# Gate and up products of a 512-token swiglu as seven block products instead of eight

## The chip, the cores and the metric

The kernel runs on one core of a Trainium2 chip. Its time is device microseconds from the first to the last instruction of one execution; several executions of a kernel are compared by their median. Five engines take part: TensorE (PE) multiplies, VectorE (DVE) and ScalarE (ACT) do the elementwise work, SyncE (SP) issues the loads, GpSimd (POOL) does next to nothing here. Each engine runs its own instructions in order and waits on semaphores for the others.

## What is computed

Two blocks of a diffusion transformer over 256 latent and 256 context tokens of width 1024, in fp32. Cut to its core:

```python
def _modulate(t, g, shift, scale):
    return _rms(t, g) * (1 + scale) + shift

def _swiglu(h, w13, w2):
    gte, up = jnp.split(h @ w13, 2, axis=-1)
    return (jax.nn.silu(gte) * up) @ w2

mod = silu(c) @ mod_w[i] + mod_b[i]             # nine vectors; another nine from c_ctx
lat = lat + 0.5 * mod[0, 2] * _swiglu(_modulate(lat, ...), ffn_w13[i, 0], ffn_w2[i, 0])
lat = lat + mod[1, 2] * mixer(_modulate(lat, ...))   # i = 0: short convolution, i = 1: attention
lat = lat + 0.5 * mod[2, 2] * _swiglu(_modulate(lat, ...), ffn_w13[i, 1], ffn_w2[i, 1])
```

The context tokens go through the same steps with their own modulation, except behind the attention. So there are three swiglus over 512 tokens, called ffn(0,0), ffn(0,1) and ffn(1,0) after layer and place, and a last one, ffn(1,1), over the 256 latent tokens. The hidden width is 2816, that is 22 tiles of 128.

## The kernel before

All activations lie with features on the partitions and tokens along the free dimension: `x` is 8 tiles (k tiles) of 128 features by 512 tokens, the latent stream in columns 0 to 255, the context in 256 to 511. An fp32 operand is split into two float32r parts: ACT copies the high part (L90), DVE subtracts it for the low part (L91). Each product is then three matmuls (`mm3`, L105 to L107): high by high, high by low, low by high.

A swiglu goes through the 22 pairs of a gate tile (`pg`) and an up tile (`pu`) in two halves of 11. For a pair SP loads 1 MB of `w13` into one of three raw buffers (`wr`), ACT and DVE split it (`wh`, `wl`), and PE runs 8 k tiles x 2 x 3 matmuls over 512 columns. Then ACT takes the silu of the gate (L357), DVE multiplies by up (L359, `gm`), and both split the product into `gh` and `gl`, an operand of the second product. After 11 pairs `project` runs the 8 output tiles of `w2` over these 11 tiles and adds them, times the gate `G`, to `x` (L296). With the last half's output, squares and sums for the norm are made as tiles come (`tail_norm`); the last two output tiles are done a stream at a time (`late`), so that the norm of the latent tokens (L222, L225, L226: `t`, `hh`, `hl`) runs behind the products of the context. Where a swiglu begins with no pair done, its first two pairs are interleaved by stream, in products of 256 columns.

The modulation vectors of all chunks but the first two are made on DVE: a job (`mod_job`) loads 1 MB of `modT` and runs four (two where only the latent stream is needed) multiply-and-reduce instructions (L128, output `junk`). There are 64 jobs in a list. `tick()` takes the next one after every other pair and every other output tile, and after each tile of the convolution; what is needed and not yet done is forced where it is first read (`mod_ready`), as by the gate of a block. The instructions stand on each engine in an order that the scheduler of the framework makes from the program's order and its own estimates; it is fixed when the kernel is built.

```python
        hi = wp.tile([P, 2048], F32R, name=nm("wh"), tag="wh", bufs=3)
        lo = wp.tile([P, 2048], F32R, name=nm("wl"), tag="wl", bufs=3)
        ...
        ticks[0] += 1
        if jobs and ticks[0] % every == 0:
            mod_job(*jobs.pop(0))
```

## Time and profile before

| | |
|---|---|
| median of 3 runs | 1619.42 us (1618.96 to 1620.31) |
| span of the profiled execution | 1618.8 us |
| PE busy | 1607.0 us (99%) |
| DVE busy | 996.7 us (62%) |
| ACT busy | 535.2 us (33%) |
| loads | 245 MB, 152 GB/s over the span |

The stages by the trace: start 0 to 62 us, ffn(0,0) to 394, convolution and its projection to 604, ffn(0,1) to 936 and its last tiles to 968, ffn(1,0) to 1300, then attention, output projection and ffn(1,1) to the end. A row of the timeline gives the start, the length, the engine, line, operation, output and inputs of an instruction; a row of waits gives who waited for whom, the total, the number of times and the longest; a row of windows gives, for a stretch, its length, then each engine's busy time and the number of its instructions, the granted clock of TensorE, the share of the DMA engines and GB/s. Matmul records overlap: what one costs is the distance to the start of the next.

### The profile page before, as it was taken

To read this page: it belongs to the slowest core of one execution; us is meant where nothing else is said; L and a number is where in the kernel's file an instruction comes from. 1 tells how busy PE (TensorE), PEld (TensorE's weight loads), DVE (VectorE), ACT (ScalarE), POOL (GpSimd) and SP (SyncE) were. 2 spreads that over 40 slices of the span, in tenths; PEclk is the share of its full clock that TensorE was granted. 3 is DMA by queue.
4 is the path that set the end of the run, shared out by engine and by line. 5 is a ranking of instruction groups with operands and counts; after the bars stand their busy time and mean duration, and the time that the engine had idled before them with its cause. 6 is when DMAs were issued, how large, how long until landed. Compare 5 with 4: busy or idle time off the path is not lost.

```text
span 1618.8 us, 21098 instructions
## 1 busy us (share of the span) xinstructions
PE 1607.0 (99%) x8718; PEld 1390.3 (86%) x8718; DVE 996.7 (62%) x1601; ACT 535.2 (33%) x811; POOL 0.2 (0%) x4
## 2 busy tenths in 40 slices
PE   9999999999999999999999999999999999999999
PEld 6888888889888898888888898888888899989999
DVE  4975565566978795557554595445443577855554
ACT  4422122224322252222222342222222356553442
POOL 0000000000000000000000000000000000000000
PEclk9999999999999999999999999999999999999999
DMA  8543544333544434345343345335433432244643
GB/s 311 213 165 124 192 163 156 132 116 131 182 163 175 177 136 152 118 138 204 130 148 124 135 154 182 124 130 207 152 124 120 161 129 84 106 156 137 218 169 103
DMA packets 40560, 248.49 MB, mean 153 GB/s; under 512 B 5392, under 2 KB 7184, under 8 KB 16656
## 3 DMA queue, kind: packets, MB, share of 16 engines
q1 hardware_dynamic: 38016, 245.38, 42.9%
q10 hardware_dynamic: 2448, 1.76, 0.4%
q8 instruction: 68, 1.11, 0.3%
q14 instruction: 28, 0.23, 0.0%
HBM read 244.77 MB, written 1.05 MB: 152 GB/s over the span
## 4 chain that ended last, share of the span: by engine, by line
PE 95%; DVE 3%; ACT 1%; DMA 1%; issue 0%; ACTq 0%; SPq 0%; DVEq 0%
PE py L105 10%; PE py L106 10%; PE py L107 10%; PE pg L105 9%; PE pg L106 9%; PE pu L105 9%; PE pu L106 8%; PE pg L107 8%; PE pu L107 8%; PE pr L434 1%; PE pv L105 1%; PE pv L107 1%; PE pv L106 1%; PE pb L107 1%; PE pb L105 1%; PE pc L107 1%
## 5 line engine op out<-in xcount | busy, mean ns | idle before, releaser
L90 ACT ACTIVATE wh<-wr 128x1024 fp32r<-128x1024 f32 (+2 forms) x358 | 326.8, 952 | 344.7 <-PE py L106 210.1
L91 DVE TENSOR_TENSOR wl<-wr,wh 128x1024 fp32r<-128x1024 f32 (+2 forms) x358 | 384.3, 1095 | 24.1 <-ACT wh L90 23.0
L128 DVE CUSTOM_DVE_ANT_0 junk<-wr,scbc,modb 128x1024 bf16<-128x1024 f32 x236 | 293.1, 1280 | 145.2 <-DMA wr<-in_modT 145.2
L107 PE MATMUL py<-gh,wl 128*128 128x512 f32 (+1 forms) x770 | 267.1, 347 | 0.0
L105 PE MATMUL py<-gh,wh 128*128 128x512 f32 (+1 forms) x770 | 267.1, 347 | 0.0
L106 PE MATMUL py<-gl,wh 128*128 128x512 f32 (+1 forms) x770 | 266.9, 347 | 0.0
L105 PE MATMUL pg<-hh,wh 128*128 128x512 f32 (+1 forms) x736 | 262.3, 356 | 2.0 <-ACT hh L225 2.0
L106 PE MATMUL pg<-hl,wh 128*128 128x512 f32 (+1 forms) x736 | 261.5, 355 | 0.0
L105 PE MATMUL pu<-hh,wh 128*128 128x512 f32 (+1 forms) x736 | 261.5, 356 | 0.0
L106 PE MATMUL pu<-hl,wh 128*128 128x512 f32 (+1 forms) x736 | 261.4, 355 | 0.0
L107 PE MATMUL pu<-hh,wl 128*128 128x512 f32 (+1 forms) x736 | 261.3, 355 | 0.0
L107 PE MATMUL pg<-hh,wl 128*128 128x512 f32 (+1 forms) x736 | 261.3, 355 | 0.0
L357 ACT ACTIVATE sg<-pg 128x512 f32<-128x512 f32 (+1 forms) x88 | 47.9, 545 | 551.1 <-PE pg L107 551.1
L359 DVE TENSOR_TENSOR gm<-sg,pu 128x512 f32<-128x512 f32 (+1 forms) x88 | 54.5, 620 | 225.0 <-ACT sg L357 213.4
L105 PEld LDWEIGHTS py<-gh,wh 128*128 128x128 f32 x770 | 145.2, 189 | 18.2
L107 PEld LDWEIGHTS py<-gh,wl 128*128 128x128 f32 x770 | 145.2, 189 | 18.0
L106 PEld LDWEIGHTS py<-gl,wh 128*128 128x128 f32 x770 | 145.2, 189 | 18.0
L105 PEld LDWEIGHTS pg<-hh,wh 128*128 128x128 f32 x736 | 139.4, 189 | 22.5 <-ACT hh L225 2.7
L105 PEld LDWEIGHTS pu<-hh,wh 128*128 128x128 f32 x736 | 139.4, 189 | 19.5
L106 PEld LDWEIGHTS pg<-hl,wh 128*128 128x128 f32 x736 | 139.1, 189 | 19.2
L107 PEld LDWEIGHTS pu<-hh,wl 128*128 128x128 f32 x736 | 139.0, 189 | 19.3
L107 PEld LDWEIGHTS pg<-hh,wl 128*128 128x128 f32 x736 | 139.0, 189 | 19.3
(155 smaller groups left out, 1608.8 us busy)
## 6 DMA issues: line engine op xcount, KB each, us to landing
wr<-in_w SPq DMA_DIRECT2D x88, 1024.0 KB, 4.8
wr<-in_modT SPq DMA_DIRECT2D x67, 1024.0 KB, 4.8
wr<-in_w SPq DMA_DIRECT2D x64, 704.0 KB, 4.1
wr<-in_cw_cx SPq DMA_DIRECT2D x8, 1024.0 KB, 4.8
wr<-in_mod SPq DMA_DIRECT2D x5, 1024.0 KB, 7.0
wr<-in_cw_b SPq DMA_DIRECT2D x4, 1024.0 KB, 4.7
wr<-in_cw_out SPq DMA_DIRECT2D x4, 1024.0 KB, 4.8
wr<-in_wq SPq DMA_DIRECT2D x4, 1024.0 KB, 4.8
```

What stands on the lines that cost most here:

```text
L90: nc.scalar.activation(out=hi, in_=src, func=AF.Copy)
L91: nc.vector.tensor_tensor(out=lo, in0=src, in1=hi.bitcast(F32), op=ALU.subtract)
L105: nc.tensor.matmul(ps, wh, mh, start=first, stop=False)
L106: nc.tensor.matmul(ps, wh, ml, start=False, stop=False)
L107: nc.tensor.matmul(ps, wl, mh, start=False, stop=last)
L128: nc.vector.tensor_tensor_reduce(out=junk, in0=raw[:, j * D : j * D + D], in1=scbc[:, v, :], scale=1.0, scalar=modb[:, l, col : col + 1], ...
L357: nc.scalar.activation(out=sg[:, :n], in_=pp[0][:, :n], func=AF.Silu)
L359: nc.vector.tensor_tensor(out=gm[:, :n], in0=sg[:, :n], in1=pp[1][:, :n], op=ALU.mult)
L434: nc.tensor.matmul(pr[:2, :S], sccol[:, k, :], raw[:, k * S : k * S + S], start=(k == 0), stop=(k == KT - 1),)
```

## The change

61 of the 66 pairs of the three 512-token swiglus (all but the first three of ffn(0,0) and the first of each of the others, which is done in two halves of 256 columns with the `head` of the next two pairs between them) are seen as a product of two by two blocks. The weight blocks are A11 (gate) and so on: rows are gate (1) and up (2), columns are k tiles 0 to 3 and 4 to 7; the activation blocks B are k tiles by stream. The Strassen-Winograd scheme needs seven block products, each of 4 k tiles x 3 matmuls x 256 columns. `Pair` makes the weight sums S1 to S4 on DVE (L519, L525, L527) from the loaded fp32 and splits A11 with A12, S1 with S2, S3 with S4 (1024 columns each) and A22 (512). The sums T1 to T4 of the activations are made once per swiglu on DVE (`Blocks.sums`; in ffn(0,0) `FirstBlocks.sums`, L341 to L345), from an fp32 copy of the normed activations that the norm now also writes.

PE runs a pair in pieces, interleaved with the pair before: `head` (two products, with A11 and A12), `five` (S1 by T1), then `seven` of the pair before (S3 by T3), `six` (S2 by T2, S4 by B22), then `four` of the pair before (A22 by T4). Partial results stay in two PSUM tiles `p` and `q`. ACT copies them to SBUF where an addend is needed (L545, L551, L555), DVE adds (L557 for the gate; L562 for up, back into PSUM), ACT takes the silu (L558), and DVE multiplies (L568).

The 22 pairs go in thirds of 8, 7 and 7, so `w2` is loaded and projected in three parts. A projection starts with three output tiles at once, whose last two k tiles wait for the last pair's `seven` and `four`, which stand between them. Weights are split into half tiles of 1024 columns with four buffers. Modulation jobs are no longer taken in the pairs: `tick(ev)` adds a share for each output tile (0.5, in ffn(1,0) 0.9; in the convolution 1.2 a tile) and takes whole jobs. The normed activations and the attention's turned tiles live in 16 buffers of 1024 columns (`hop`).

On DVE, the steady loop of the pairs in the second half of ffn(0,0) before, and in the second third now (`gm`: the pair's product, `gl`: its low part, `wl`: low parts of weights, `ws`: weight sums, `w4l`: that of A22, `p`: the up sum, `sg`: the gate sum):

```order
L359 TENSOR_TENSOR gm_1696<-sg_1694,pu_1645 128x512
L91 TENSOR_TENSOR wl_1856<-wr_1853,wh_1855 128x1024
L91 TENSOR_TENSOR gl_1643<-gm_1696,gh_1642 128x512
L91 TENSOR_TENSOR wl_1856<-wr_1853,wh_1855 128x1024
L128 ISA junk_1993,mod_4_1700<-wr_1985,scbc,modb 128x1024
L128 ISA mod_4_1700 128x1
L359 TENSOR_TENSOR gm_1773<-sg_1771,pu_1722 128x512
L91 TENSOR_TENSOR wl_1922<-wr_1919,wh_1921 128x1024 x2
L91 TENSOR_TENSOR gl_1720<-gm_1773,gh_1719 128x512
```

After the change, at the same place:

```order
L562 TENSOR_TENSOR p_1987<-p_1987,gm_2027 128x256
L92 TENSOR_TENSOR wl_2217<-ws_2209,wh_2216 128x1024
L92 TENSOR_TENSOR wl_2222<-ws_2209,wh_2221 128x1024
L557 TENSOR_TENSOR sg_2110<-q_2109,sg_2110 128x512
L519 TENSOR_TENSOR ws_2330<-wr_2328 128x2x512
L568 TENSOR_TENSOR gm_2027<-sg_1989,p_1987 128x512
L92 TENSOR_TENSOR w4l_2226<-wr_2207,w4h_2225 128x512
L525 TENSOR_TENSOR ws_2330<-wr_2328,ws_2330 128x512
L92 TENSOR_TENSOR gl_2191<-gm_2027,gh_2190 128x512
L527 TENSOR_TENSOR ws_2330<-wr_2328,ws_2330 128x512
L92 TENSOR_TENSOR wl_2332<-wr_2328,wh_2331 128x1024
```

The modulation is gone from the loop; three weight sums, two more low parts and two sums of results have come into it, eleven rows to a pair.

On DVE, in the projection after the first part of ffn(0,0) (`x`: an output tile's addition; `junk`: modulation):

```order
L296 SCALAR_TENSOR_TENSOR x<-py_1282,G_1215,x 128x256 x2
L91 TENSOR_TENSOR wl_1419<-wr_1416,wh_1418 128x768
L91 TENSOR_TENSOR wl_1419<-wr_1416,wh_1418 128x640
L296 SCALAR_TENSOR_TENSOR x<-py_1326,G_1215,x 128x256 x2
L91 TENSOR_TENSOR wl_1473<-wr_1470,wh_1472 128x768
L91 TENSOR_TENSOR wl_1473<-wr_1470,wh_1472 128x640
L128 ISA junk_1560,mod_3_1263<-wr_1558,scbc,modb 128x1024
...
L128 ISA junk_1562,mod_3_1263<-wr_1558,scbc,modb 128x1024
...
L128 ISA junk_1564,mod_3_1263<-wr_1558,scbc,modb 128x1024
...
L128 ISA junk_1566,mod_3_1263<-wr_1558,scbc,modb 128x1024
...
L296 SCALAR_TENSOR_TENSOR x<-py_1380,G_1215,x 128x256 x2
```

After the change, at the same place:

```order
L417 SCALAR_TENSOR_TENSOR x<-py_1447,G_1418,x 128x256 x2
L138 ISA junk_1476,mod_3_1427<-wr_1474,scbc,modb 128x1024
...
L92 TENSOR_TENSOR wl_1487<-wr_1484,wh_1486 128x1024
L138 ISA junk_1478,mod_3_1427<-wr_1474,scbc,modb 128x1024
...
L92 TENSOR_TENSOR wl_1518<-wr_1484,wh_1517 128x1024
L138 ISA junk_1480,mod_3_1427<-wr_1474,scbc,modb 128x1024
...
L138 ISA junk_1482,mod_3_1427<-wr_1474,scbc,modb 128x1024
...
L138 ISA junk_1550,mod_3_1427<-wr_1548,scbc,modb 128x1024
...
L417 SCALAR_TENSOR_TENSOR x<-py_1490,G_1418,x 128x256 x2
L138 ISA junk_1552,mod_3_1427<-wr_1548,scbc,modb 128x1024
...
L138 ISA junk_1554,mod_3_1427<-wr_1548,scbc,modb 128x1024
...
L92 TENSOR_TENSOR wl_1561<-wr_1558,wh_1560 128x1024
```

Before, the four rows of a job stand behind the weights of every second output tile. Now rows of jobs stand around every low part of the weights (`wl_1487` and the others); eight jobs lie in this projection, of which the gate `G` forces the first four.

On DVE, at the start of the attention (`wl_9527` before and `wl_12935` now are the first query weights):

```order
L296 SCALAR_TENSOR_TENSOR x<-py_9257,G_7894,x 128x256 x2
L91 TENSOR_TENSOR wl_9527<-wr_9524,wh_9526 128x1024 x2
L192 TENSOR_TENSOR acc_9034<-acc_9034,sq_9293 128x256
...
L296 SCALAR_TENSOR_TENSOR x<-py_9315,G_7894,x 128x256
...
L296 SCALAR_TENSOR_TENSOR x<-py_9353,G_7894,x 128x256
L210 RECIPROCAL ri_9416<-rs_9414 128x2
L222 SCALAR_TENSOR_TENSOR t_9420<-x,A_9390,ss_9409 128x256
...
L226 SCALAR_TENSOR_TENSOR hl_6937<-t_9420,mod_3_6182,hh_6936 128x256
...
L296 SCALAR_TENSOR_TENSOR x<-py_9393,G_7894,x 128x256
```

After the change, at the same place:

```order
L138 ISA junk_12911,mod_8_12900<-wr_12907,scbc,modb 128x1024
...
L231 SCALAR_TENSOR_TENSOR t_12827<-x,A_12803,ss_12816 128x256
...
L242 SCALAR_TENSOR_TENSOR hl_9154<-t_12827,mod_3_10288,hh_9153 128x256
...
L417 SCALAR_TENSOR_TENSOR x<-py_12806,G_10284,x 128x256
...
L417 SCALAR_TENSOR_TENSOR x<-py_12859,G_10284,x 128x256
...
L242 SCALAR_TENSOR_TENSOR hl_9160<-t_12881,mod_3_10288,hh_9159 128x256
L138 ISA junk_12915,mod_8_12900<-wr_12913,scbc,modb 128x1024
...
L92 TENSOR_TENSOR wl_12935<-wr_12932,wh_12934 128x1024
L138 ISA junk_12917,mod_8_12900<-wr_12913,scbc,modb 128x1024
...
L92 TENSOR_TENSOR wl_12937<-wr_12932,wh_12936 128x1024
```

The query weights stood ahead of the norm's rows; now they stand behind the norm of the latent stream and behind three rows of the last modulation chunk, and the fourth and fifth come next.

The diff, cut to its core:

```diff
-HALF = NM // 2
+THIRDS = (8, 7, 7)
...
-    gp = ctx.enter_context(tc.tile_pool(name="gp", bufs=12))
+    hop = ctx.enter_context(tc.tile_pool(name="hop", bufs=16))
+    gp = ctx.enter_context(tc.tile_pool(name="gp", bufs=8))
...
+    def half():
+        return tuple(
+            wp.tile([P, 1024], F32R, name=nm(t), tag=t, bufs=4) for t in ("wh", "wl")
+        )
...
-    def tick(every=2):
...
-        ticks[0] += 1
-        if jobs and ticks[0] % every == 0:
+    owed = [0.0]
+    def tick(share):
+        owed[0] += share
+        while jobs and owed[0] >= 1:
+            owed[0] -= 1
             mod_job(*jobs.pop(0))
...
+    class Blocks:
...
+        def block(self, s, hf, A, B, ri, fine=False):
+            raw = self.raw[hf, s] = hot("hr", F32)
+            hi, lo = self.t["B", hf, s] = hot("bh"), hot("bl")
+            for i in range(4):
+                k = 4 * hf + i
+                c = slice(i * S, i * S + S)
+                t = scaled(s, k, A, ri)
+                nc.scalar.activation(
+                    out=raw[:, c], in_=t, func=AF.Identity, bias=B[:, k, s : s + 1]
+                )
+                if fine and i % 2:
+                    c = slice((i - 1) * S, (i + 1) * S)
+                    split(hi[:, c], lo[:, c], raw[:, c])
+            if not fine:
+                split(hi, lo, raw)
...
+        def sums(self):
+            r = self.raw
+            b11, b12, b21, b22 = r[0, 0], r[0, 1], r[1, 0], r[1, 1]
+            tt = nc.vector.tensor_tensor
+            def keep(key, src):
+                hi, lo = self.t[key] = hot("th"), hot("tl")
+                split(hi, lo, src)
+            tt(out=b11, in0=b12, in1=b11, op=ALU.subtract)
+            keep("T1", b11)
+            tt(out=b12, in0=b22, in1=b12, op=ALU.add)
+            tt(out=b22, in0=b22, in1=b11, op=ALU.add)
+            keep("T2", b22)
+            tt(out=b21, in0=b21, in1=b22, op=ALU.subtract)
+            keep("T3", b12)
+            keep("T4", b21)
...
+        nf = 3 if between else 2
+        w2 = [ws(m) for m in range(nf)]
+        p2 = [psum("py") for _ in range(nf)]
+        cut = nk - 2 if between else nk - 1
+        for i in range(nf):
+            products(p2[i], w2[i], range(cut), 0, tot)
+            if i < len(between):
+                between[i]()
+        if between:
+            for i in range(nf):
+                products(p2[i], w2[i], (nk - 2,), 0, tot)
+        for i in range(nf):
+            products(p2[i], w2[i], (nk - 1,), 0, tot)
+            finish(i, p2[i], 0, tot, gate, tail)
+            tick(ev)
...
+    class Pair:
+        def __init__(self, src, h):
+            self.h = h
+            raw = load_raw(src)
+            a21, a22, a11, a12 = (raw[:, i * T2 : i * T2 + T2] for i in range(4))
+            tt = nc.vector.tensor_tensor
+            sm = wp.tile([P, 2048], F32, name=nm("ws"), tag="ws", bufs=1)
+            s1, s2, s3, s4 = (sm[:, i * T2 : i * T2 + T2] for i in range(4))
+            self.w = {}
+            def keep(keys, src):
+                hi, lo = half()
+                split(hi, lo, src)
+                for i, key in enumerate(keys):
+                    self.w[key] = [t[:, i * T2 : i * T2 + T2] for t in (hi, lo)]
+            keep(("A11", "A12"), raw[:, 1024:])
+            tt(
+                out=sm.rearrange("p (a b c) -> p a b c", a=2, b=2)[:, :, 0, :],
+                in0=a21.unsqueeze(1).to_broadcast([P, 2, T2]),
+                in1=raw[:, T2 : 3 * T2].rearrange("p (a c) -> p a c", a=2),
+                op=ALU.subtract,
+            )
+            tt(out=s2, in0=a11, in1=s1, op=ALU.subtract)
+            keep(("S1", "S2"), sm[:, :1024])
+            tt(out=s4, in0=a12, in1=s2, op=ALU.subtract)
+            keep(("S3", "S4"), sm[:, 1024:])
+            self.w["A22"] = [
+                wp.tile([P, T2], F32R, name=nm(t), tag=t, bufs=2) for t in ("w4h", "w4l")
+            ]
+            split(*self.w["A22"], a22)
+        def prod(self, ps, wk, hk, first=True):
+            for k in range(4):
+                w = tuple(t[:, k * P : k * P + P] for t in self.w[wk])
+                mm3(ps, w, self.h.blk(hk, k), first and k == 0, k == 3, True)
+        def head(self):
+            p, q = psum("p"), psum("q")
+            self.p, self.q, self.q1 = p[:, :S], q, q[:, S:]
+            self.u = p
+            self.sg = tp.tile([P, T2], F32, name=nm("sg"), tag="sg", bufs=3)
+            self.prod(self.p, "A11", ("B", 0, 0))
+            nc.scalar.copy(self.sg[:, :S], self.p)
+            self.prod(q[:, :S], "A12", ("B", 1, 0))
+        def five(self):
+            self.prod(self.q1, "S1", "T1")
+            self.gm = tp.tile([P, T2], F32, name=nm("gm"), tag="gm", bufs=3)
+            nc.scalar.copy(self.gm[:, S:], self.q1)
+        def six(self):
+            self.prod(self.p, "S2", "T2", False)
+            nc.scalar.copy(self.sg[:, S:], self.p)
+            self.prod(self.q1, "S4", ("B", 1, 1), False)
+            nc.vector.tensor_tensor(out=self.sg, in0=self.q, in1=self.sg, op=ALU.add)
+            nc.scalar.activation(out=self.sg, in_=self.sg, func=AF.Silu)
+        def seven(self):
+            self.prod(self.p, "S3", "T3", False)
+            nc.vector.tensor_tensor(
+                out=self.u[:, S:], in0=self.p, in1=self.gm[:, S:], op=ALU.add
+            )
+        def four(self, g):
+            self.prod(self.p, "A22", "T4", False)
+            nc.vector.tensor_tensor(out=self.gm, in0=self.sg, in1=self.u, op=ALU.mult)
+            split(g[0], g[1], self.gm)
...
+    def ffn(l, b, h, tot, gate, tail, gs=(), ev=0.5):
         gs = list(gs)
-        for hf in range(2):
-            m0 = hf * HALF
-            if hf == 0 and tot == T2 and not gs:
-                ws = [load_w(a["w13"][l, b, i]) for i in range(2)]
-                gs = [new_pair("g") for _ in range(2)]
-                pps = [(psum("pg"), psum("pu")) for _ in range(2)]
...
-            for i in range(len(gs), HALF):
-                w = load_w(a["w13"][l, b, m0 + i])
-                gs.append(new_pair("g"))
-                pp = psum("pg"), psum("pu")
-                w13_mm(pp, w, h, range(KT), 0, tot)
-                w13_post(pp, gs[i], 0, tot)
-                tick(ev)
+        i0 = 0
+        for t, n in enumerate(THIRDS):
+            between = ()
+            if tot == T2:
+                heads = []
+                if t == 0 and not gs:
+                    w = load_w(a["w13"][l, b, 0])
+                    gs = [new_pair("g")]
+                    pp = psum("pg"), psum("pu")
+                    w13_mm(pp, w, h, range(KT), 0, S)
+                    flush()
+                    for i in (1, 2):
+                        heads.append(Pair(a["w13"][l, b, i], h))
+                        heads[-1].head()
+                    w13_mm(pp, w, h, range(KT), S, T2)
+                    w13_post(pp, gs[0], 0, T2)
+                prev = None
+                for i in range(len(gs), n):
+                    if heads:
+                        pr = heads.pop(0)
+                    else:
+                        pr = Pair(a["w13"][l, b, i0 + i], h)
+                        pr.head()
+                    pr.five()
+                    if prev:
+                        prev.seven()
+                    pr.six()
+                    if prev:
+                        gs.append(new_pair("g"))
+                        prev.four(gs[-1])
+                    prev = pr
+                def last():
+                    gs.append(new_pair("g"))
+                    prev.four(gs[-1])
+                between = (prev.seven, last)
...
+                    src = a["w2a"][l, b, m // 2] if t == 0 else a["w2b"][l, b, t - 1, m // 2]
+                    box[m // 2] = load_raw(src, 2 * n * P)
...
-        tick(1)
+        tick(1.2)
...
-    hn = new_h()
-    ffn(1, 0, h, T2, lazy_gate(1, 0), tail_norm(1, 1, hn))
...
+    hn = Plain()
+    ffn(1, 0, h, T2, lazy_gate(1, 0), tail_norm(1, 1, hn), (), 0.9)
```

312 lines of the change are left out of this document (187 added, 125 removed).

## The prediction

> **What bounds the kernel now.** I read the page first, for the engine that sets the end, then the waits of TensorE (PE), then the groups by form, and last the timeline for the spacing of single instructions.
>
> ```profile
> PE 1607.0 (99%) x8718; PEld 1390.3 (86%) x8718; DVE 996.7 (62%) x1601; ACT 535.2 (33%) x811; POOL 0.2 (0%) x4
> PE 95%; DVE 3%; ACT 1%; DMA 1%; issue 0%; ACTq 0%; SPq 0%; DVEq 0%
> PE pg L105 <- ACT hh L225: 2.0, 2, 1.1
> PE ss L212 <- DVE ri L210: 1.5, 1, 1.5
> ```
>
> PE is busy for 1607.0 of 1618.8 us and is 95% of the chain that ended last; its longest wait group is 2.0 us. PE is the bound everywhere, so the time is its matmuls, and any new stall of PE adds in full. The sum is made against the profiled span of 1618.8 us; the runs' median is 1619.42, so I add 0.6 at the end and round.
>
> In the windows by stage, VectorE (DVE) has much idle time beside each of the three large swiglus (the last three rows; the first is the kernel's start):
>
> ```profile
> 0.00:62.00 62.00, 59.64 (x303) 42.16 (x304) 39.57 (x87) 27.13 (x45) 0.20 (x4) 0.97 0.78 280
> 62.00:394.00 332.00, 331.08 (x1504) 275.64 (x1503) 202.28 (x306) 91.72 (x129) 0.00 (x0) 1.00 0.43 152
> 604.00:936.00 332.00, 332.00 (x1508) 276.66 (x1506) 191.73 (x286) 88.03 (x121) 0.00 (x0) 1.00 0.42 146
> 968.00:1300.00 332.00, 332.00 (x1508) 276.67 (x1506) 159.10 (x229) 87.54 (x121) 0.00 (x0) 1.00 0.43 152
> ```
>
> The columns are PE, weight loads, DVE, ScalarE (ACT) and POOL, then PE's granted clock (1.00). DVE is busy 202, 192 and 159 of 332 us. That idle time pays for the change.
>
> **The gain on PE.** Matmul records overlap (0.39 us each), so their cost is the spacing of their starts (the first number of a row; the second is the record's length):
>
> ```profile
> 299.75 0.39 PE L106 MATMUL pu<-hl,wh 128*128 128x512 f32 x1
> 302.93 0.39 PE L105 MATMUL pg<-hh,wh 128*128 128x512 f32 x1
> 1499.77 0.28 PE L106 MATMUL py<-gl,wh 128*128 128x256 f32 x1
> 1502.88 0.28 PE L105 MATMUL py<-gh,wh 128*128 128x256 f32 x1
> ```
>
> Between the first two lie 14 intervals: 3.18 / 14 = 0.227 us for 512 columns. Between the other two lie 26: 3.11 / 26 = 0.1196 us for 256. A pair now is 48 matmuls of 512, 10.90 us; as seven block products it is 7 x 4 x 3 = 84 of 256, 10.05 us. The seven-eighths saving (1.36) shrinks to 0.85 since 84 short matmuls pay their fixed part more often. Over the whole program the 512-column matmuls go from 5106 to 2346 and the 256-column ones from 3180 to 7968: -2760 x 0.2271 + 4788 x 0.1196 = -626.8 + 572.6 = **-54.2 us**. (It is more than 61 x 0.85 because ffn(0,1) and ffn(1,0) no longer open with two interleaved tiles, whose products were 256 wide.) Their weight loads come one per matmul as now, at the spacing of the 256-column rows.
>
> The Trainium skill (TensorE: Matmul & The Clock Gate, section "Wait — 56ns, not 53.3ns?") puts the spacing at N / 2.4 GHz plus some 2.5 ns. By that the gain would be -2760 x 0.2158 + 4788 x 0.1092 = -72.8, an estimate; the rows' own fixed part is 2 x 0.1196 - 0.2271 = 0.012 us, and the sum goes by the rows.
>
> **What the change puts on DVE.** The costs are again spacings:
>
> ```profile
> 304.32 1.28 DVE L128 CUSTOM_DVE_ANT_0 junk<-wr,scbc,modb 128x1024 bf16<-128x1024 f32 x1
> 305.53 1.28 DVE L128 CUSTOM_DVE_ANT_0 junk<-wr,scbc,modb 128x1024 bf16<-128x1024 f32 x1
> 307.34 1.22 DVE L91 TENSOR_TENSOR wl<-wr,wh 128x1024 fp32r<-128x1024 f32 x1
> 308.47 0.68 DVE L91 TENSOR_TENSOR gl<-gm,gh 128x512 fp32r<-128x512 f32 x1
> 309.07 1.22 DVE L91 TENSOR_TENSOR wl<-wr,wh 128x1024 fp32r<-128x1024 f32 x1
> 1304.55 0.48 DVE L226 SCALAR_TENSOR_TENSOR hl<-t,mod,hh 128x256 fp32r<-128x256 f32 x1
> 1304.95 0.42 DVE L192 TENSOR_TENSOR acc<-acc,sq 128x256 f32<-128x256 f32 x1
> 1305.28 0.87 DVE L222 SCALAR_TENSOR_TENSOR t<-x,A,ss 128x256 f32<-128x256 f32 x2
> ```
>
> So a modulation row ("junk") takes 1.21, 1024 elements 1.13, 512 take 0.60, 256 take 0.33, and the scalar form over 256 takes 0.40. A block-product pair has three 1024-wide low parts and the double sum L519 (4 x 1.13), L525, L527, the low part of A22, L557, L568 and the pair's own low part (6 x 0.60) and L562 (0.33): **8.5 us on DVE against 10.05 on PE**. ACT has 5.3 (its 1024 rows take 1.05). In the steady loop nothing stalls PE as I walk it: the u sum (L562) follows `seven`, and PE does two more blocks (2.9 us) before `four` needs it; the first half of the next pair's weights takes the buffer that `head` has left. That cover is thin, though: DVE keeps 1.5 us a pair, where before its rows of a pair were 2 x 1.13 + 2 x 0.60 = 3.5 of 10.90 with only modulation in the rest.
>
> DVE as a whole goes from 997 busy to about 1313 by the same spacings, under PE's 1607 - 54 = 1553. The trouble sits in places where DVE's rows bunch. I compare DVE's rows with PE's matmuls between two points where both must meet:
>
> (1) Start of ffn(0,0). The last low part of the norm leaves DVE at 66.26 and PE reaches the fourth pair 5.5 us later:
>
> ```profile
> 65.86 0.48 DVE L226 SCALAR_TENSOR_TENSOR hl<-t,mod,hh 128x256 fp32r<-128x256 f32 x1
> 71.73 0.39 PE L105 MATMUL pg<-hh,wh 128*128 128x512 f32 x1
> ```
>
> Now 17 rows of 512 (T sums and their low parts, three gm, three gl) and the weights' first half come after it and ahead of the fourth pair: 17 x 0.60 + 1.13 = 11.3. That is 5.8 us late; the double sum and low parts behind it, which `five` waits for, and a later last norm row add 2.7: **8.5**, bounds 7 to 10.
>
> (2) First third's projection in ffn(0,0). The gate of that block forces its four modulation jobs at once, and ticks add four more. From the u sum of pair 6 to that of the next third's first pair DVE has 32 junk (38.6), 17 of 1024 (19.2), 12 of 512 (7.2), 16 scalar (6.3) and 2 u sums (0.7): 72.0 us. PE has 192 x 0.227 + 14 blocks x 1.435 = 63.7. The difference is 8.3; PE may be 2.9 ahead at the end (least 5.5), and the loads can add: 15 of these stretch over three buffers,
>
> ```profile
> wr<-in_modT SPq DMA_DIRECT2D x67, 1024.0 KB, 4.8
> ```
>
> which at 4.8 us one after another is 72 us too (most 13). I take **10**, since m = 4's weights stand behind 21 junk rows.
>
> (3) The same in ffn(1,0), with 32 junk, 16 of 1024, 12 of 512, 16 scalar: 70.9 against 63.7. **9**, bounds 4.5 to 11.
>
> (4) Starts of ffn(0,1) and ffn(1,0). The norm now also writes fp32 blocks and forms T1 to T4 after the second stream. DVE has 32.4 us from the last latent product to the first u sum, and PE 31.7, but DVE first waits for the norm's scale as it does now:
>
> ```profile
> 588.40 1.26 DVE L222 SCALAR_TENSOR_TENSOR t<-x,A,ss 128x256 f32<-128x256 f32 x3 [1.69 <-PE ss L212]
> ```
>
> Two such waits (3.4) and 0.7 are 4.1; I take **4.5** and, with a shorter tail of products as cover in ffn(1,0), **5**; bounds 1 to 6 each.
>
> (5) Attention's start. Before, the query weights stand ahead of the norm on DVE, and PE goes straight on. Now four jobs are forced there: from the last latent product on, DVE has 19 scalar rows (7.5), 3 junk (3.6), 2 square sums (0.7) and the weights (1.1) to do ahead of the first query product, 13.1 with small rows; PE has 5.7 us of context products left then. **8** with the hand-over, bounds 7 to 9.
>
> (6) Conv's start 1, the remaining thirds (DVE 53.2 to 58.8 against PE 58.2 to 63.7) 1, short waits of the pairs' hand-overs 2 (bounds 0 to 7). Waits of before that vanish: 1 off at most.
>
> Sum of losses: 8.5 + 10 + 9 + 9.5 + 8 + 4 - 1 = 48, bounds 31 to 62. Removed at no other cost: the modulation rows in the pairs only move, and the number of bytes of w2 stays. 1618.8 - 54.2 + 48 = 1612.6, plus 0.6: **1613 us**, and by the bounds 1596 to 1627.
>
> **Rivals.** (A) The stalls are mostly hidden: PE takes the gain nearly whole. For it: DVE's total is 85% of PE's, and idle PE time at one place may let later rows run ahead. Against: buffers let DVE run ahead by one pair only, and the gates force their jobs at fixed places. With 20 of 48 lost: 1585.
>
> (B) DVE becomes the bound of the pair loop, and the kernel is slower. Price: if rows cost their full records (1.22, 0.68, 0.42) a pair is 4 x 1.22 + 6 x 0.68 + 0.42 = 9.4, and three of them start only after PE's result, with some 0.3 us each in which DVE is idle: 10.35 a pair. Over 52 pairs in steady state 0.3 x 52 = 16: 1628. It decides from 10.05 a pair on. Against it stand the rows above, which start 1.13 and 0.60 apart without a wait.
>
> (C) Gaps of PE slow the clock. Before shows PE at clock 1.00 through all three swiglus without a gap above 2 us, and 0.97 over the first 62 us, which begin from standstill: 62 x 0.03 = 1.9 us lost. If each of some five gaps of 5 us or more makes PE start over in that way, they cost 5 x 1.9 = 9 more: 1622. The Trainium skill (TensorE: Matmul & The Clock Gate, section "HAM oscillation — how this bites in real kernels") states this rule: an idle stretch above some 3.4 us puts the array back to half clock until it has been busy for as long; that would be 1.7 a gap, an estimate near the row's 1.9. The trace of before has no such gap and cannot show it.
>
> (D) The change does not save: short matmuls in alternation of many weights run slower than 0.1196. The final swiglu's rows alternate just so; 0.125 would undo half of the gain (84 x 61 x 0.0054 = 28): 1640.
>
> **How the numbers follow.** Forecast 0.44, A 0.20, B 0.12, C 0.21, D 0.03. What counts as no change is within 0.2%, 3.2 us (1616.2 to 1622.7). Of the forecast 0.29 lies below, 0.10 within, 0.05 above; A is all below; B 0.01 within, 0.11 above; C 0.04 below, 0.09 within, 0.08 above; D above. Faster 0.53, same 0.20, slower 0.27. The forecast's own range is 1596 to 1627; most of A and B reach beyond it, so I give 1588 to 1630, which leaves out the lower half of A, D and part of B.
>
> **What would show it.** Right: PE busy near 1553, in the steady pairs no wait of PE above 0.1, pairs 10.05 us apart, and idle PE of 5 to 10 us at the start of each large swiglu, in the first thirds' projections (released by DVE wl) and ahead of the first pq, 40 to 55 in all. B would show as pairs 10.3 apart with DVE idle nowhere; C as a granted clock under 1.00 behind the gaps, with matmuls 0.24 apart; A as idle PE under 25 in all. The forecast is wrong if the projections' junk rows run while PE has no gap.

## The result, and the profile after

The changed kernel takes 1635.05 us (median; 1633.68 to 1636.17) where the kernel before takes 1619.34 in the same comparison: ratio 1.0091, 95% interval 1.0076 to 1.0105. A later comparison on the same footing gave 1.0087 (1.0074 to 1.0100). The forecast was 1613 with a range of 1588 to 1630: the change is slower, not faster.

The head of the page, busy time by engine and the chain that ended last:

```profile
PE 1581.4 (97%) x10746; PEld 1463.5 (90%) x10746; DVE 1358.5 (83%) x2066; ACT 735.1 (45%) x1131; POOL 0.2 (0%) x4
...
PE 85%; DVE 10%; DMA 2%; ACT 1%; issue 1%; DVEq 0%; ACTq 0%; SPq 0%
```

PE's share of the chain fell from 95% to 85%, and DVE's rose from 3% to 10%. DVE is busy 1358 us instead of 997. PE's busy time fell by 26 only, but it also counts the slower matmuls in stretches of low clock, so it isn't the gain. The gain is seen where nothing disturbs: the second third of ffn(0,0), first as a window (columns as before), then two successive starts of `head`, twelve matmuls of A11 by B11 each:

```profile
297.00:364.90 67.90, 67.90 (x567) 67.86 (x566) 57.48 (x72) 37.71 (x58) 0.00 (x0) 1.00 0.31 106
...
314.47 0.28 PE L115 MATMUL p<-hh,wh 128*128 128x256 f32 x1
...
324.55 0.28 PE L115 MATMUL p<-hh,wh 128*128 128x256 f32 x1
```

A pair takes 324.55 - 314.47 = 10.08 us, against 10.05 forecast and 10.90 as a plain pair. PE has no idle time in 67.9 us, while DVE is busy for 57.5 of them.

The loss is seen in the waits of PE (who waited for whom, total, times, longest):

```profile
PE p L117 <- DVE wl L92: 8.6, 3, 5.0
PE pg L115 <- ACT bh L91: 6.1, 2, 3.0
PE py L117 <- DVE wl L92: 5.9, 2, 3.5
PE py L115 <- ACT wh L91: 4.6, 1, 4.6
PE pg L115 <- ACT hh L241: 3.9, 2, 2.8
PE pq L117 <- DVE wl L92: 3.4, 2, 2.3
```

All waits together are 49.3 us (8.7 before), most of them a few long ones: low parts of weights (`wl`), or the split of the context's norm (`bh`). Around most of these waits the granted clock falls. Windows around the five worst places of the changed kernel:

```profile
75.00:100.00 25.00, 19.99 (x147) 19.79 (x147) 23.55 (x30) 13.11 (x20) 0.00 (x0) 0.86 0.25 85
150.00:180.00 30.00, 23.03 (x88) 17.78 (x87) 28.41 (x48) 4.02 (x4) 0.00 (x0) 0.83 0.50 176
590.00:620.00 30.00, 26.18 (x199) 25.32 (x199) 25.81 (x32) 20.10 (x30) 0.00 (x0) 0.94 0.18 59
1080.00:1100.00 20.00, 15.78 (x125) 14.99 (x124) 19.29 (x26) 9.28 (x15) 0.00 (x0) 1.00 0.51 181
1300.00:1345.00 45.00, 36.44 (x213) 33.59 (x213) 36.01 (x69) 21.57 (x37) 0.00 (x0) 0.85 0.57 203
```

In the first, second and fourth, DVE is busy for 94 to 96% of the stretch and PE for 77 to 80%. In the fourth the clock stays at 1.00 in spite of a wait of 3.4 us.

To place the whole difference I took, from the trace, the distance of every matmul's start to the next one's. What exceeds 0.227 us (512 columns) or 0.120 (256) is loss, counted as a wait where the profile shows PE idle, as low clock where half the clock was granted, and else as small. A distance that holds idle time counts as a wait in full, so the sum of waits lies somewhat above the 49.3. Over the whole span:

```
                         before    after   difference
matmuls at full spacing  1594.9   1543.1      -51.8
waits                       9.7     54.7      +45.0
low clock                   3.8     19.6      +15.8
small                       6.1     12.3       +6.2
first and last 4 us         4.4      4.4        0.0
sum                      1618.9   1634.1      +15.2
```

and by place, loss only, beside the terms of the forecast:

```
                                          before  after  more   forecast
ffn(0,0) to its second third's pairs        6.9   30.2   23.3   18.5 (terms 1 and 2)
starts of ffn(0,1) and ffn(1,0)             0.2   14.6   14.4    9.5 (term 4)
ffn(1,0), first projection and after       -0.3   10.7   11.0    9   (term 3)
ffn(1,0)'s end to the output projection    10.2   26.7   16.5    8   (term 5)
everything else                             2.6    4.4    1.8    3   (term 6)
sum                                        19.6   86.6   67.0   48
```

The first row of the upper table is worked out and not timed: the number of matmuls of each width times the spacing, which is 0.120 in the pairs above (10.08 / 84). PE's busy time shows it only with low clock and small excess (-51.8 + 15.8 + 6.2 = -29.8, beside the 26 above).

So the gain came (52 of 54), and losses of 67 us instead of 48 used it up. By kind, the waits alone are 45.0 more, near the 48; low clock and small excess are the rest. Nearly every loss lies where it was expected.

How a loss looks: the fifth output tile of the first projection, with the issue of its load (SPq), ACT's high part and DVE's timeline, and after them PE's two waits there (in brackets the idle time before a row and what ended it):

```profile
153.33 0.33 SPq L87 DMA_DIRECT2D wr<-in_w2a  x1
...
158.18 2.00 ACT L91 ACTIVATE wh<-wr 128x1024 fp32r<-128x1024 f32 x2 [15.20 <-DMA wr<-in_w2a]
...
157.80 1.28 DVE L138 CUSTOM_DVE_ANT_0 junk<-wr,scbc,modb 128x1024 bf16<-128x1024 f32 x1
...
159.39 1.28 DVE L138 CUSTOM_DVE_ANT_0 junk<-wr,scbc,modb 128x1024 bf16<-128x1024 f32 x1
...
161.38 1.28 DVE L138 CUSTOM_DVE_ANT_0 junk<-wr,scbc,modb 128x1024 bf16<-128x1024 f32 x1
...
162.58 1.23 DVE L92 TENSOR_TENSOR wl<-wr,wh 128x1024 fp32r<-128x1024 f32 x1
163.72 1.28 DVE L138 CUSTOM_DVE_ANT_0 junk<-wr,scbc,modb 128x1024 bf16<-128x1024 f32 x1
...
159.29 0.80 PE L115 MATMUL py<-gh,wh 128*128 128x512 f32 x1 [4.57 <-ACT wh L91]
163.86 0.79 PE L117 MATMUL py<-gh,wl 128*128 128x512 f32 x1 [2.40 <-DVE wl L92]
```

The first wait ends with ACT's high part of these weights, and ACT had waited for their load. That load was issued at 153.33 only, when DVE was through the sixteen rows of the four forced jobs, the last of which starts at 152.01: the jobs' data and the weights share the three raw buffers. The low part runs at 162.58, behind modulation rows and the tiles' additions without a gap, and PE goes on at 163.86. The two matmuls' records are 0.80 and 0.79 us long instead of 0.39: half clock.

### The profile page after: what moved, and what is told of

The parts are those of the page before. It is cut to its first block, busy times and chain, and to the rows that moved or that the text cites. A ratio compares the mean times of both kernels' runs of the same rounds, so it can differ in the third digit from the quotient of the medians.

```text
span 1634.1 us, 26052 instructions
## 1 busy us (share of the span) xinstructions
PE 1581.4 (97%) x10746; PEld 1463.5 (90%) x10746; DVE 1358.5 (83%) x2066; ACT 735.1 (45%) x1131; POOL 0.2 (0%) x4
## 4 chain that ended last, share of the span: by engine, by line
PE 85%; DVE 10%; DMA 2%; ACT 1%; issue 1%; DVEq 0%; ACTq 0%; SPq 0%
PE py L115 8%; PE py L117 8%; PE py L116 8%; PE p L117 7%; PE p L115 7%; PE p L116 7%; PE q L117 5%; PE q L115 5%; PE q L116 5%; DVE junk L138 4%; DVE wl L92 2%; PE pg L116 2%; PE pg L115 2%; PE pg L117 2%; PE pu L116 2%; PE pu L117 2%
## 5 line engine op out<-in xcount | busy, mean ns | idle before, releaser
L92 DVE TENSOR_TENSOR wl<-ws,wh 128x1024 fp32r<-128x1024 f32 x122 | 148.7, 1223 | 30.0 <-ACT wh L91 29.7
L117 PEld LDWEIGHTS py<-gh,wl 128*128 128x128 f32 x746 | 142.0, 190 | 26.7 <-DVE wl L92 7.3
L91 ACT ACTIVATE wh<-ws 128x1024 fp32r<-128x1024 f32 x122 | 128.3, 1058 | 81.9 <-PE p L116 37.6
L116 PE MATMUL p<-tl,wh 128*128 128x256 f32 x488 | 138.2, 283 | 0.0
L115 PE MATMUL p<-th,wh 128*128 128x256 f32 x488 | 138.2, 283 | 0.0
L117 PE MATMUL p<-th,wl 128*128 128x256 f32 x488 | 137.8, 283 | 0.0
L115 PE MATMUL q<-bh,wh 128*128 128x256 f32 x336 | 95.2, 283 | 0.4 <-ACT gm L551 0.4
L116 PE MATMUL q<-bl,wh 128*128 128x256 f32 x336 | 95.2, 283 | 0.0
L117 PE MATMUL q<-bh,wl 128*128 128x256 f32 x336 | 95.1, 283 | 0.0
L116 PEld LDWEIGHTS p<-tl,wh 128*128 128x128 f32 x488 | 93.8, 192 | 0.3
L115 PEld LDWEIGHTS p<-th,wh 128*128 128x128 f32 x488 | 93.8, 192 | 0.3
```

What stands on the lines that cost most here:

```text
L91: nc.scalar.activation(out=hi, in_=src, func=AF.Copy)
L92: nc.vector.tensor_tensor(out=lo, in0=src, in1=hi.bitcast(F32), op=ALU.subtract)
L115: nc.tensor.matmul(ps, wh, mh, start=first, stop=False, **kw)
L116: nc.tensor.matmul(ps, wh, ml, start=False, stop=False, **kw)
L117: nc.tensor.matmul(ps, wl, mh, start=False, stop=last, **kw)
```

## The experiments

Theory A: VectorE's rows bunch at a few places (modulation forced or ticked there, sums, norm), PE waits for weights or the norm behind them, and its clock falls with the waits. Rivals: the loss is spread over the block pairs (B); the low clock by itself is what was not foreseen (C); the new thirds and projections cost by themselves. (These letters are the experiments' own, not those of the prediction.)

**The idle stretches filled.** Products that nobody reads are put into the waits:

```diff
+    def fill(ps, n):
+        for _ in range(n):
+            nc.tensor.matmul(ps[:, :P], ones, ones, start=True, stop=True)
...
+            if m == 4:
+                fill(ps, {(0, 0, 0): 30, (1, 0, 0): 16}.get(here[0], 0))
```

> The changed kernel, with products that nobody reads (128 columns of ones, about 0.22 us each) put into TensorE's longest idle stretches: 30 and 16 ahead of the fifth output tile of the first projections of ffn(0,0) and ffn(1,0), 21 and 14 ahead of the first block pair there, 13 ahead of the context half of the first pair of ffn(0,1) and ffn(1,0), 9, 5 and 9 ahead of the query products. The waits for data stay. Theory A (the clock falls to half because of the idle stretches, and that costs 16 us beside the 45 of waits): most of the half-clock stretches (51 us in all after the change, 10 before) are gone, and of the 16 us those come back that lie where TensorE and not VectorE sets the pace: 1624 to 1630 us. Rival (the low clock costs nothing, since TensorE waits there anyway): 1633 to 1637.

Measured: 1634.63 us, ratio 1.0093 (1.0073 to 1.0114), beside 1.0087 (1.0074 to 1.0100) for the changed kernel: no difference that can be measured. Three windows of the filled kernel, to be read beside those above:

```profile
590.00:620.00 30.00, 28.40 (x228) 27.22 (x227) 26.63 (x33) 19.96 (x30) 0.00 (x0) 1.00 0.20 70
1300.00:1345.00 45.00, 39.70 (x265) 37.05 (x264) 36.45 (x67) 23.55 (x39) 0.00 (x0) 0.92 0.54 188
150.00:180.00 30.00, 27.54 (x145) 23.45 (x144) 28.57 (x48) 4.02 (x4) 0.00 (x0) 0.94 0.50 178
```

The clock there rose from 0.94, 0.85 and 0.83 to 1.00, 0.92 and 0.94, and the low-clock loss of the whole profile fell from 19.6 to 8.5. But waits and filling together rose from 54.7 to 61.2, and the span fell by 3.6 us only (1634.1 to 1630.5), of which 1.4 lie ahead of the first filled place (the same matmul starts at 64.81 and at 63.38). Behind most of the filling PE still waited for data (0.34 us at 78.97, 2.46 at 162.88, 0.79 at 600.12), so there the filling didn't hold it up. The slow matmuls mostly run while DVE is late anyway: with a faster clock PE arrives earlier and waits longer. The rival's reading is nearer. The low clock is real and lies around the waits, but as a price of its own I can show only some 2 of its 16 us.

**A plain first third.** In ffn(0,0) the other five pairs of the first third are plain, so that the projection behind them begins with two output tiles instead of three:

```diff
+                    if not heads and i in PLAIN.get((l, b, t), ()):    # PLAIN = {(0, 0, 0): (3, 4, 5, 6, 7)}
+                        w = load_w(a["w13"][l, b, i0 + i])
...
+                        w13_mm(pp, w, h, range(KT), 0, T2)
```

> The changed kernel, with the remaining five pairs of the first third of ffn(0,0) done as plain products. TensorE pays 5 x 0.82 = 4.1 us, VectorE has 25 us less to do there. Theory A (the losses are waits at the few places where VectorE's rows bunch, and the clock behind them): the waits at 159 to 192 us (7.7) and the half clock behind them (2.7) go, the one at 80 us stays: 1628, between 1625 and 1631. Rival (the loss is spread over the block pairs): 5 of 61 of the loss of 67 is 5.5, less 4.1: 1633.

Measured: 1625.76 us, ratio 1.0032 (1.0021 to 1.0044), 9 us under the changed kernel for 4 us more of products. From the start to the second third's pairs the loss falls from 30.2 to 15.2. The waits at 159 to 192 us are gone but for 0.5, as theory A has it, and the one at 80 (5.0) shrank as well to two of 1.4 and 1.1, which I had not expected. Five block pairs less, 5 of 61, take away 15 of 67 us of loss: it isn't spread evenly over the pairs.

**No block products.** All pairs plain, everything else of the change kept:

```diff
-                    if not heads and i in PLAIN.get((l, b, t), ()):
+                    if True:
...
-    hn = Blocks()
+    hn = Plain()
...
-    h = FirstBlocks(h, h32)
-    h.sums()
```

> The changed kernel without any block product: all 66 pairs plain, no sums of weights or activations, but w2 still in three parts, the modulation still only in the projections, the same buffers. Theory A (part of the loss is the moved modulation, whatever the products are): the attention's start still waits (9.1 and 5.4 of low clock, against 1.2 before), little else: 1632, between 1626 and 1636. Rival (all of the loss comes from the block products' load on VectorE): 1617 to 1621, the time before.

Measured: 1627.23 us, ratio 1.0044 (1.0029 to 1.0059). So some 7 of the 16 us that the changed kernel lies above the one before come without any block product. The loss by place, in a profiled execution 5 us above the median, is 20.4 at the attention, 10 more than before, and 9.1 at the start, but nothing in the two other swiglus. Something of the change costs at the attention whatever the products are: the moved modulation, the thirds or the buffers, which this run doesn't separate.

**Short modulation rows.** Each modulation row takes 128 columns instead of 1024 (the modulation vectors, and so the outputs, are then not those of the reference):

```diff
-                    out=junk,
-                    in0=raw[:, j * D : j * D + D],
-                    in1=scbc[:, v, :],
+                    out=junk[:, :P],
+                    in0=raw[:, j * D : j * D + P],
+                    in1=scbc[:, v, :P],
```

> The changed kernel, whose modulation rows multiply and reduce only 128 of their 1024 columns, so that the modulation vectors are wrong; all loads and all instructions stay. It takes about 1 us off each of 236 rows on VectorE. Theory A (modulation rows that stand ahead of weights make the waits in the first projections and at the attention's start): 7.7 and 7.4 of waits and 4.3 of low clock in the projections go, and about 9 of the 14.5 at the attention; the starts of the swiglus keep theirs: 1606, between 1602 and 1614. Rival (the waits come from the weight sums and the loads): 1625 to 1634.

Measured: 1591.78 us, ratio 0.9825 (0.9809 to 0.9841), some 43 us under the changed kernel and 14 better than I expected. Its page and its longest waits:

```profile
PE 1567.1 (99%) x10746; PEld 1455.3 (92%) x10746; DVE 1157.3 (73%) x2066; ACT 737.2 (46%) x1131; POOL 0.2 (0%) x4
...
PE pg L115 <- ACT bh L91: 6.1, 2, 3.0
PE ss L212 <- ACT sq L195: 2.6, 2, 1.6
```

No wait for weights (`wl`, `wh`) is left among the long ones; the longest is 0.96 us, for `wh` at the query weights. Loss by place: start to second third 4.9 (30.2 in the changed kernel), first projection of ffn(1,0) and after 0, attention 18.6 (26.7); the starts of ffn(0,1) and ffn(1,0) keep theirs (6.8 and 8.6), for these wait for the norm (`bh`, the first row of waits). What I had missed is the start: twelve modulation rows lie there as well, ahead of the T sums, and without their length the wait at 80 us goes too.

**The last modulation chunk later.**

```diff
-    mod_ready(1, 8)
+    mod_ready(1, 7)
...
-    mp = modctx.enter_context(tc.tile_pool(name="mp", bufs=2))
+    mp = ctx.enter_context(tc.tile_pool(name="mp", bufs=2))
+    sp = modctx.enter_context(tc.tile_pool(name="sp", bufs=1))
```

> The changed kernel, with one thing moved: the last chunk of the modulation (four jobs of two rows each, the gate of the last swiglu) is not forced ahead of the attention but made where the last swiglu first needs it. (The weight sums' tile lies in a pool that ends before the attention, so that the modulation's vectors can stay.) Theory A (rows of that chunk stand ahead of the query weights and make the waits at the attention's start): of 26.7 us that TensorE loses between the end of ffn(1,0) and the output projection some 8 go, as in the run with short modulation rows: 1627, between 1624 and 1630. Rival (the query weights are late because they stand behind the norm, whatever the chunk): 1632 to 1636.

Measured: 1630.46 us, ratio 1.0056 (1.0037 to 1.0075): 4 to 5 us under the changed kernel by the medians, 3 by the profiles. The attention's loss falls from 26.7 to 14.9, more than expected, but the last swiglu's first projection now loses 4.6, ffn(1,0)'s last 3.2 (0.7 in the changed kernel). A part of the rows' lateness only moved.

**Weight sums on GpSimd.**

```diff
-            tt(out=s2, in0=a11, in1=s1, op=ALU.subtract)
+            nc.gpsimd.tensor_tensor(out=s2, in0=a11, in1=s1, op=ALU.subtract)
```

(and S1 with S3, and S4, in the same way)

> The changed kernel, with the weight sums S1 to S4 (1.13 and 2 x 0.60 us a pair on VectorE) made on GpSimd instead. Theory A (VectorE's bunched rows set the losses): 2.3 us a pair less for VectorE, in the two first projections' stretches 3 and 2 pairs, so 7 and 5 us of waits go, and some of the low clock behind them: 1622, between 1617 and 1629. Rival (GpSimd needs more than 3 us for a row, or hinders VectorE, and the products wait for the sums): 1640 or more, with waits in every pair.

Measured: 1672.28 us, ratio 1.0319 (1.0303 to 1.0334): the rival's forecast came. Groups by form, of GpSimd's sums, of two of DVE's low parts and of its u sum's row L557 in this run, then the same three of DVE in the changed kernel:

```profile
L519 POOL TENSOR_TENSOR ws<-wr 128x1024 f32<-128x1024 f32 x61 | 157.0, 2573 | 910.0 <-DMA wr<-in_w 386.4 <-DVE wl L92 247.2 <-DVE x L417 213.9
L525 POOL TENSOR_TENSOR ws<-wr,ws 128x512 f32<-128x512 f32 x61 | 105.9, 1736 | 4.8
...
L92 DVE TENSOR_TENSOR w4l<-wr,w4h 128x512 fp32r<-128x512 f32 x61 | 87.2, 1433 | 0.5 <-ACT w4h L91 0.5
L92 DVE TENSOR_TENSOR gl<-gm,gh 128x512 fp32r<-128x512 f32 x66 | 82.3, 1250 | 2.5 <-ACT gh L91 2.4
L557 DVE TENSOR_TENSOR sg<-q,sg 128x512 f32<-128x512 f32 x61 | 41.6, 681 | 0.0
```

```profile
L92 DVE TENSOR_TENSOR gl<-gm,gh 128x512 fp32r<-128x512 f32 x66 | 45.2, 687 | 2.6 <-ACT gh L91 2.6
...
L92 DVE TENSOR_TENSOR w4l<-wr,w4h 128x512 fp32r<-128x512 f32 x61 | 41.8, 685 | 0.0
L557 DVE TENSOR_TENSOR sg<-q,sg 128x512 f32<-128x512 f32 x61 | 41.8, 685 | 2.7 <-PE q L117 2.6
```

A sum of 1024 takes 2.57 us on GpSimd against 1.22 on DVE. And DVE's own low parts of 512 take 1.43 and 1.25 us on average instead of 0.69, while L557, one of whose inputs (`q`) comes from PSUM, keeps its 0.68. Told apart row by row in the trace, the low parts of 512 that overlap a GpSimd sum take 1.72 us and the others 0.68 to 0.69; those of plain weights with 1024 take 2.27 and 1.22. The Trainium skill (SBUF — State Buffer, section "SBUF: two separate sides") says that VectorE and GpSimd share a pair of ports as an exclusive lock, and that a VectorE row with two SBUF inputs needs it beside a GpSimd row that reads SBUF, as these sums do; the rows that grew and the one that didn't agree. DVE's busy time rose (1358 to 1385) although it lost 183 rows.

**More cover at the starts.** ffn(0,1) and ffn(1,0) begin with two plain pairs and one block pair's `head` ahead of the context half:

```diff
-                    w = load_w(a["w13"][l, b, 0])
...
-                    for i in (1, 2):
+                    ws = [load_w(a["w13"][l, b, i]) for i in range(2)]
...
+                    for i in range(2, 3):
                         heads.append(Pair(a["w13"][l, b, i], h))
                         heads[-1].head()
...
```

> The changed kernel, with ffn(0,1) and ffn(1,0) beginning with two plain pairs by stream and one block pair's first two products ahead of the context half, instead of one plain pair and two block pairs. That is 2.9 us more work of TensorE that needs the latent tokens alone, for 1.45 us more in all a swiglu (96 x 0.12 against 84 x 0.12). Theory A (there TensorE waits for the context's norm, split and sums): of the 6.8 and 7.8 us lost at the two starts some 8 go, and the 5 us less on VectorE take some 3 off the first projection of ffn(1,0): 1634 - 8 + 3 - 3 = 1626, between 1622 and 1630. Rival (VectorE is behind as a whole there, so more cover changes nothing): 1634 to 1638.

Measured: 1628.87 us, ratio 1.0048 (1.0033 to 1.0062), beside 1.0087 for the changed kernel on the same chip, whose run is this:

> The changed kernel itself, beside the others on the same chip: 1635, ratio 1.007 to 1.011.

The starts' loss falls from 14.6 to 4.6, for 3 us more of products. The starts lacked cover for the context's norm, as theory A says: two blocks' worth of further products ahead of it (2.9 us) take 10 of the 14.6 away. The first projection of ffn(1,0) kept its 11 us or so (4.1 and 7.7), so the five microseconds of DVE that a plain pair saves did not help there.

**Everything spread.** One kernel with the plain third, the two-pair starts, a further plain pair in ffn(1,0), T sums one pair later, modulation shares of 0.6, 0.75, 0.75 and 0.5, 0.75, 0.75 in the thirds of ffn(0,1) and ffn(1,0), and the late last chunk (of the diff, its two tables):

```diff
+EV = {(0, 1, 0): 0.6, (0, 1, 1): 0.75, (0, 1, 2): 0.75, (1, 0, 0): 0.5, (1, 0, 1): 0.75, (1, 0, 2): 0.75}
+PLAIN = {(0, 0, 0): (3, 4, 5, 6, 7), (1, 0, 0): (3,)}
```

> A version that should beat both, by theory A: block products as in the change, but the first third of ffn(0,0) and a third pair of ffn(1,0) plain; ffn(0,1) and ffn(1,0) begin with two plain pairs by stream and one block pair's first products (2.9 us more work ahead of the context norm); more modulation jobs in the projections of ffn(0,1) (shares 0.6, 0.75, 0.75) and fewer in ffn(1,0) (0.5, 0.75, 0.75); T1 to T4 of ffn(0,0) one pair later; the last chunk in the last swiglu. By the losses of the single runs: 1635 - 9 (first third) - 8 (attention) - 10 (first projection of ffn(1,0)) - 12 + 4 (starts and plain pairs) = 1600, between 1592 and 1610. If the losses do not add up, since one bound takes the place of another: 1612 to 1625.

Measured: 1609.97 us (1604.25 to 1610.52), ratio 0.9928 (0.9909 to 0.9948): faster than both kernels. Its page and longest waits:

```profile
PE 1575.3 (98%) x10602; PEld 1450.6 (91%) x10602; DVE 1316.2 (82%) x2010; ACT 713.7 (45%) x1091; POOL 0.2 (0%) x4
...
PE pg L119 <- ACT hh L245: 3.9, 2, 2.7
PE q L119 <- ACT wh L95: 3.4, 1, 3.4
PE py L119 <- ACT wh L95: 2.3, 2, 1.9
```

The profiled span (1602.5) lies near the 1600 that the sum of the single runs gave; that execution took 1604.25, and the median is 6 us above it, at the upper end of what was expected. All losses together are 46.9, against 86.6 in the changed kernel.

> The version before this one, with the weight sums on GpSimd as well. Theory A: VectorE is nowhere the bound any more but at the start, so little is left to gain: 0 to 5 us under the version without it, 1597. Rival (GpSimd's rows are slow or hinder VectorE): some us to some tens of us above it.

With the weight sums on GpSimd (the same edit as above) it takes 1637.77, ratio 1.0108 (1.0093 to 1.0123): 28 us worse than without.

**Spread further.** Shares of 0.5 and 0.95 in the last thirds of ffn(0,1) and ffn(1,0), and the last chunk in the attention's output projection:

```diff
-EV = {..., (0, 1, 2): 0.75, ..., (1, 0, 2): 0.75}
+EV = {..., (0, 1, 2): 0.5, ..., (1, 0, 2): 0.95}
...
-lazy_gate(1, 1), tail_norm(1, 2, hn), S, 0, 0,
+lazy_gate(1, 1), tail_norm(1, 2, hn), S, 0, 0.5,
```

> The version with everything spread (1609.97, profile 1602.5), with its three remaining places of bunched modulation moved: the share in the last third of ffn(0,1) is 0.5 (there TensorE waited 3.4 us for weights at 817 us and 1.1 at 908), that in the last third of ffn(1,0) 0.95, and the last chunk is made in the attention's output projection (0.5) instead of the last swiglu's first projection (1.9 of wait at 1460). Theory A: 5.4, 1.7 and 2.9 us of loss go: 1594 in the profile, ratio 0.985 to 0.990. Rival (the rows find another place to be late): the time stays near the version before.

Measured: 1613.11 us, ratio 0.9950 (0.9938 to 0.9962), no better than the version before it. The 1.7 and 2.9 us at 908 and 1460 went, but the attention's loss rose from 17.0 to 26.3 and the one at 817 us stayed (3.4 of wait). That wait isn't due to the share I had blamed. And the eight rows of the moved chunk run between 1330 and 1388 us, amid the attention's own products and ahead of the projection that they were meant for. The rows found another place to be late.

**What the block products are worth.** The kernel without block products, with the last chunk late:

```diff
-    mod_ready(1, 8)
-    modctx.close()
+    mod_ready(1, 7)
```

> The kernel without any block product (w2 in thirds, modulation in the projections alone), with the last modulation chunk made in the last swiglu. It lost 20.4 us at the attention's start and lies 7 us above the kernel before. Theory A (its only loss is the modulation ahead of the query weights): 1620, within 3 us of the kernel before, and so the version with block products and the rows spread (ratio 0.993) owes its gain to the block products. Rival (thirds and hoisted modulation cost elsewhere too): 1624 to 1628; or, if the spreading alone is the gain, 1608 to 1614.

Measured: 1629.88 us, ratio 1.0055 (1.0041 to 1.0068), no gain over 1.0044. The attention's loss fell from 20.4 to 15.5; the last swiglu's first projection lost 2.6, and in the profiled start PE waits 2.9 us at 18 us, where it waited 1.0 before. That is slower than I expected of theory A, and I can't name a cause for the whole of the remainder. But the kernel without block products is no faster than the one before. It hasn't the shares of the spread version, so spreading without block products is not tested in full. That the 0.993 comes from the products is seen in the spread version's own sum: 1602.5 less losses of 46.9 and 4.4 at the ends leaves some 1551 us of matmuls at full spacing, 44 less than before, while its losses are 27 more.

## Why the prediction was wrong, point by point

- **The gain on PE** (-54.2): right. By the counts it is -51.8 at the measured spacing of 0.120, where 0.1196 was forecast; pairs are 10.08 us apart. Rival D (short matmuls slower in alternation) is refuted. PE's busy time is 1581 and not near the 1553 that was to show it, since it counts the low clock and the small excess too.
- **No stall in the steady pairs**: right. The windows of undisturbed pairs show no idle time; one wait of 0.39 us, for ACT's copy `gm`, is left at 1200 us. Rival B, DVE as the bound of the pair loop, is refuted, though DVE's margin is as thin as stated: 57.5 of 67.9 us.
- **Where it loses**: right, but for a few microseconds behind the query weights, and the idle time of PE, 49.3 us, is inside the 40 to 55 that were said to show it. Rival A is refuted.
- **The size of the loss**: wrong, and this is the step that failed. But for term 6, the sum's 48 are waits of PE alone, each walked at full clock to the first point where the engines meet. Measured by place the loss is 67, and the upper bound of 62 was too low as well. By kind, the waits are 45.0 more; the low clock around them, at nothing in the sum and 9 in rival C, is 15.8; the small excess over full spacing is 6.2, where term 6 had 2. These are not separate prices: with the clock mostly kept up, waits and filling are 61.2, 51.5 more than before, and the median is the same. So, as I read it, a part of DVE's lateness shows as slow matmuls instead of waits; how much of the missing 19 is the clock's own stays open.
 - *Attention* (term 5): 8 forecast, 16.5 measured. The waits up to the second query weights are 8.6; the low clock around them adds some 4, and some 2 lie behind, in the attention's own products (1.0 us each for `e` and `ptl`), which no term named. The sum stopped at the first half of the first query weights. Behind it the rest of the query weights is late as well, as DVE's and PE's timelines show:

```profile
1311.65 1.28 DVE L138 CUSTOM_DVE_ANT_0 junk<-wr,scbc,modb 128x1024 bf16<-128x1024 f32 x1
1312.86 1.22 DVE L92 TENSOR_TENSOR wl<-wr,wh 128x1024 fp32r<-128x1024 f32 x1
...
1322.03 1.26 DVE L231 SCALAR_TENSOR_TENSOR t<-x,A,ss 128x256 f32<-128x256 f32 x3 [2.87 <-PE ss L223]
1323.21 1.22 DVE L92 TENSOR_TENSOR wl<-wr,wh 128x1024 fp32r<-128x1024 f32 x1
...
1310.08 0.39 PE L115 MATMUL pq<-hh,wh 128*128 128x256 f32 x1 [2.04 <-ACT wh L91]
1314.14 0.58 PE L117 MATMUL pq<-hh,wl 128*128 128x256 f32 x1 [1.12 <-DVE wl L92]
1324.48 0.39 PE L117 MATMUL pq<-hh,wl 128*128 128x256 f32 x1 [2.26 <-DVE wl L92]
```

   The second query weights stand on DVE behind rows of the context's norm, which wait 2.87 us for PE's sums, and these in turn come late from PE. So a wait that I counted once comes round a second time, 2.26 us.
 - *Starts of ffn(0,1) and ffn(1,0)* (term 4): 9.5 forecast, 14.4 measured, of which 7.7 are waits and 3 low clock. I had priced DVE's rows up to the first u sum. PE stops earlier, at the context half of the first pair, for the split `bh` of a block that ACT makes only after all four of its k tiles (3.0 us), and again for its low part (0.8).
 - *ffn(0,0)* (terms 1 and 2): 18.5 forecast, 23.3 measured, of which 15.5 are waits and some 7 low clock. The wait ahead of the first block pair, 5.0, is near the 5.8 of the walk. The one at the last norm rows grew from 0.9 to 2.8, as two modulation rows now stand among them (60.92 and 62.53 us): with short modulation rows it is gone, and with the T sums a pair later (the spread version) it stays at 2.7.
 - *ffn(1,0)'s first projection* (term 3): 9 forecast, 11.0 measured, of which 7.4 are waits, right in size.
- **Rival C, the clock**: that gaps slow the clock was right. The trace has 51 us at half clock where there were 10, and 16 us of PE's loss in them, not 9. But the filled run shows only some 2 of them reaching the end; the others pass while DVE is late. So C does not make up the missing 19 us by itself. The Trainium skill (TensorE: Matmul & The Clock Gate, section "HAM oscillation — how this bites in real kernels") names gaps above some 3.4 us; here one wait of 2.8 us, and two of 3.0 with one of 0.8 close behind each, were enough, each with 3.4 us of half clock, and the measurement decides. The length of a wait doesn't settle it either: one of 3.40 us at 1084 left the clock at 1.00, and one of 3.21 at the same place in the kernel's second profile brought 3.4 us of half clock. Nor is the 0.97 of the first 62 us before the change a start from standstill: the granted clock is 1.00 from 5 to 15 us and 0.57 from 15 to 19.
- **The range** ended at 1630, since the bounds of the terms were put around waits at full clock. Two small slips bear on nothing here: the terms' lower bounds add up to less than the 31 given (25 to 28), and the parts of the chances to 0.54 faster and 0.19 same, not 0.53 and 0.20.

## What to carry to other kernels

Fewer matmuls are a gain only if the engine that prepares operands has room at the narrowest place, not on average: DVE was busy for 83% of the span, but for 94 to 96% where its rows bunched, and there PE waited. Price a place until both engines meet again, with second waits and slow matmuls included. A cheaper product with dearer operands belongs where the operand engine is idle, and the plain one elsewhere: 53 block pairs and spread jobs gave 0.993, where 61 gave 1.009.

## What was not expected of the hardware

- What GpSimd beside VectorE costs: 183 sums moved there made VectorE busier by 27 us (1358 to 1385), since rows with two SBUF inputs took longer beside a GpSimd sum: the two kinds of low parts shown there grew by 0.56 and 0.75 us each on average, and those of plain weights (1024 elements, 193 of them) from 1.22 to 1.54.
- A granted clock of half came with waits of 2.8 and 3.0 us, and before the change already with three of 1.1 to 1.5 within 5 us (1418 to 1423), but not with one of 3.4 at 1084. At half clock matmuls of 256 columns started 0.213 us apart, of 512 0.427.
- Filling the idle stretches with products that nobody reads raised the mean granted clock from 0.984 to 0.994, and changed the time by nothing that can be measured.
